# One token tile's attention input: transposes on the tensor engine replaced by transposing transfers, and the attention bias asked for behind them

## The chip, the cores and the metric

The kernel runs on one core of a Trainium2 chip. A core has five engines with an instruction stream each: TensorE (PE in the profile; PEld is its weight load), VectorE (DVE), ScalarE (ACT), GpSimd (POOL) and SyncE (SP), which issues most transfers. Each stream is worked off in order, and an instruction whose input is missing holds up all that stand behind it on its engine. Transfers run on 16 DMA engines. The metric is the device time of one launch in microseconds, as the median of several runs.

## What is computed

A trunk of two layers over 256 tokens of width 1024: each layer is a feed-forward part, a mixer and a second feed-forward part, each between two root-mean-square norms, on a residual stream h. The mixer of the first layer is a gated linear recurrence, that of the second an attention whose keys, values and forget-gate sums come from the stream after the first layer. Cut to the second layer:

```python
f = swiglu(rms_norm(h, ffn1_pre_g[1]), ffn1_w_gate[1], ffn1_w_up[1], ffn1_w_down[1])
h = h + 0.5 * rms_norm(f, ffn1_post_g[1])
hn = rms_norm(h, mix_pre_g[1])
m = forgetting_attention(hn, attn_w_q[0], attn_w_o[0], k, v, c)
h = h + rms_norm(m, mix_post_g[1])

def forgetting_attention(xq, w_q, w_o, k, v, c):
    q = (xq @ w_q).reshape(Bn, S, 16, 64).transpose(0, 2, 1, 3) * 64 ** -0.5
    ...
    logits = q_block @ k^T + c_query - c_key, masked to earlier tokens
    p = softmax(logits); o = p @ v
    return o.reshape(Bn, S, 1024) @ w_o
```

## The kernel before

**Tiles and operands.** The 256 tokens are two tiles t = 0 and 1 of 128, and h is kept as two tiles with tokens on the partitions. A product needs its input with features on the partitions: eight k tiles of 128 features each, for each token tile. float32 precision is reached by splitting every operand into a rounded high part and the remainder: a step of a product is three matmuls, high by high, high by low, low by high. The two parts of the current input are `xhi` and `xlo` (k tile, token), those of the weights `whi` and `wlo`. A weight is loaded into one of five `raw` buffers by SP (lines 161 and 164), rounded by ScalarE (line 173) and subtracted by VectorE (line 177); the subtraction frees the buffer.

**The order of work.** All weight pieces are a list of items. An item has a preparation (load and split) and its work for t = 0 and for t = 1, called halves. TensorE runs what is emitted in the order of emission. The other engines' streams are put together by a scheduler from readiness and priority (`tc.high_priority()` makes instructions urgent; inside one such region each engine keeps the order of emission), except that `tc.keep_in_program_order(x)` ties x behind the instruction that was emitted last before it on the same engine. After each half comes `tick()`: it counts down the list `pend`, where `defer(n, f)` puts f to be called at the (n + 1)th tick from there, and it prepares a further item.

**Into a stage.** `enter(t, ...)` stands at the end of a stage: it norms the product, adds it to h (line 311) and readies the next stage's input. For the stage looked at here, the attention's query product after the second layer's first feed-forward part, `inputs()` is deferred by `wait=3` and runs, for t = 1, after the third query half of t = 0. It transposes the eight 128 x 128 blocks of h on TensorE into two PSUM banks (`to_tp`, line 226), multiplies them by the gain (line 234), copies them to `xhi` (line 235) and subtracts for `xlo` (line 240), each in two pieces of four k tiles; `stat(t)` then forms the row norm (lines 205, 198, 200).

At other places in the kernel the second four k tiles take another way (`by_transfer`). `planes` (line 212, GpSimd) sorts the 32-bit words into two planes of 16-bit halves, `swap` (line 216) turns them with a transposing transfer on SP, in program order, and `join` (line 220, GpSimd) puts the halves together again. `turned_to_x` (lines 258, 259 and 240) makes the two operands, the multiplication and the high copy in program order.

**Attention.** Its order is written out by hand in `ATT_ORDER`:

```python
ATT_ORDER = ("0 0 0 0 0 0 0 l0 0 1 n0 l0 1 1 t0 n0 1 l0 v0 1 t0 n0 l0 1 v0 n0 1 t0 l1 1 ...
```

A digit is a half of t = 0 or t = 1; the first eight halves of each are the query product (items of two k tiles each, four items for the first eight heads, then four for the rest). `l0` are logits of tile 0: the step computes those of eight heads, adds the bias and takes the row maxima (VectorE, lines 1203 to 1208), and takes eight exponentials (ScalarE, line 1210); `n` norms them, `t` transposes them (line 1223) and `v` multiplies by the values (line 1237). After the fourth half the queries of the first heads are scaled (`heads_T`, line 1044, tile `htok`). For t = 0 they are turned on TensorE (line 1057, copied at line 1059), two ticks later; for t = 1 they are turned by planes, swap and join (lines 212, 216, 220), and the first `l1` needs them. Tile 1's bias `bias1`, 2 MB in SBUF, is read by `l1` only. It is loaded from DRAM by GpSimd's queue in `att_rows`, called just ahead of the first query half.

Of the kernel before, what the change touches and what calls it, by code (L numbers as in the profile page):

```python
# [9 lines left out]
F32 = mybir.dt.float32  # L10
F32R = mybir.dt.float32r
BF16 = mybir.dt.bfloat16
U16 = mybir.dt.uint16
AF = mybir.ActivationFunctionType
# [3 lines left out]
P = 128  # L18
# [25 lines left out]
def trunk_kernel(ctx: ExitStack, tc: tile.TileContext, A: dict, out: bass.AP):  # L44
    nc = tc.nc
# [5 lines left out]
    hpool = ctx.enter_context(tc.tile_pool(name="h", bufs=1))  # L51
# [6 lines left out]
    def nm(s):  # L58
        uid[0] += 1
        return f"{s}_{uid[0]}"  # L60
# [4 lines left out]
    def gtbank():  # L65
        return psum.tile([P, 512], F32, tag="gt", name=nm("gt"), bufs=2)
# [14 lines left out]
    def defer(n, fn):  # L81
        pend.append([n, fn])
# [23 lines left out]
    h = [hpool.tile([P, D], F32, tag=f"h{t}", name=f"h{t}") for t in range(2)]  # L106
# [23 lines left out]
    gT = cpool.tile([P, 56], F32, name="gT")  # L130
# [64 lines left out]
    def rstd_of(ss, n, f=1.0, add=nc.gpsimd):  # L195

        v = spool.tile([P, 1], F32, tag="nv", name=nm("nv"))
        add.tensor_scalar(v, ss[:, 0:1], ss[:, 1:2] if n == 2 else 0.0, D * EPS * f * f, ALU.add, ALU.add)  # L198
        r = spool.tile([P, 1], F32, tag="rstd", name=nm("rstd"), bufs=8)
        nc.gpsimd.tensor_tensor(r, v, mhalf, ALU.pow)  # L200
        return r

    def square_sum(src, acc, f=1.0):
        junk = spool.tile([P, D], BF16, tag="junk", name=nm("junk"), bufs=1)
        nc.scalar.activation(junk[:, :src.shape[1]], src, AF.Square, scale=f, accum_out=acc)  # L205

    def new_ss():
        return spool.tile([P, 2], F32, tag="ss", name=nm("ss"))

    def planes(dst, src):  # L210

        nc.gpsimd.tensor_copy(dst.rearrange("p (h f) -> p h f", h=2), src.bitcast(U16).rearrange("p (f h) -> p h f", h=2))

    def swap(turned, halves):

        tc.keep_in_program_order(nc.sync.dma_start(turned.rearrange("p (a b) -> p a b", b=P), halves, transpose=True))

    def join(dst, turned):

        nc.gpsimd.tensor_copy(dst, turned.rearrange("p (h f) -> p h f", h=2))  # L220

    def to_tp(src, n):

        tp = gtbank()
        for j in range(4):
            nc.tensor.transpose(tp[:, j * P:(j + 1) * P], src[:, n * 512 + j * P:n * 512 + (j + 1) * P], ident)  # L226
        return tp
# [10 lines left out]
    def x_lower(xg, dest, n):  # L238
        gi, xh, xl = dest
        nc.vector.tensor_tensor(xl[:, 4 * n:4 * n + 4, :], xg, xh[:, 4 * n:4 * n + 4, :].bitcast(F32), ALU.subtract)  # L240

    def to_x(tps, dest):

        with tc.high_priority():
            xg = [x_upper(tp, dest, n) for n, tp in enumerate(tps)]
            for n, v in enumerate(xg):
                x_lower(v, dest, n)

    def turned_to_x(v, dests, more):

        with tc.high_priority():
            xs = []
            for i, (gi, xh, xl) in enumerate(dests):
                xg = v if i == len(dests) - 1 else more()
                g = gT[:, gi + 4:gi + 8].unsqueeze(2).to_broadcast([P, 4, P])
                xs.append(xg.rearrange("p (a b) -> p a b", a=4))
                tc.keep_in_program_order(
                    nc.vector.tensor_tensor(xs[i], v.rearrange("p (a b) -> p a b", a=4), g, ALU.mult))
                tc.keep_in_program_order(nc.scalar.activation(xh[:, 4:, :], xs[i], AF.Copy))
            for xg, dest in zip(xs, dests):  # L260
                x_lower(xg, dest, 1)

    def to_x_tiles(tps, dest):

        gi, xh, xl = dest

        def operands(k):
            return tps[k // 4][:, k % 4 * P:(k % 4 + 1) * P], gT[:, gi + k:gi + k + 1]
        with tc.high_priority():
            for k in range(8):  # L270
                src, g = operands(k)
                nc.scalar.activation(xh[:, k, :], src, AF.Copy, scale=g)
            for k in range(8):
                src, g = operands(k)
                nc.vector.scalar_tensor_tensor(xl[:, k, :], src, g, xh[:, k, :].bitcast(F32), ALU.mult, ALU.subtract)
# [4 lines left out]
    def stat(t):  # L280
        ss = new_ss()
        square_sum(h[t], ss[:, 0:1])
        rs[t] = rstd_of(ss, 1)

    def enter(t, dests, pf, gb, half, last=False, normed=False, wait=3, spare=None):

        f = 1.0 / 16 if half else 1.0 / 32
        ss = new_ss()
        t1 = []
        urgent = tc.high_priority()  # L290
        urgent.__enter__()
        for n in range(2):
            square_sum(pf[n], ss[:, n:n + 1], f)
        for n in range(2):
            if n == 1 and last:
                r = rstd_of(ss, 2, f, nc.vector)
            t1.append(hpool.tile([P, 512], F32, tag="t1", name=nm("t1"), bufs=2))
            nc.vector.tensor_tensor(t1[n], pf[n], gb[:, n * 512:(n + 1) * 512], ALU.mult)
        if not last:
            r = rstd_of(ss, 2, f)  # L300

        sp, aq = nc.sync, nc.scalar
        pieces = [(n * 512, 512, None) for n in range(2)]
        if last:
            pieces = ([(0, 1024, sp)] if t == 0 else
                      [(0, 256, sp), (256, 256, aq), (512, 256, sp), (768, 256, aq)])
        for c, m, q in pieces:
            hn = h[t][:, c:c + m]
            for a in range(c, c + m, 512):
                n = min(m, 512)  # L310
                nc.vector.scalar_tensor_tensor(h[t][:, a:a + n], t1[a // 512][:, a % 512:a % 512 + n], r[:, 0:1],
                                               h[t][:, a:a + n], ALU.mult, ALU.add)
            if last:
                q.dma_start(out[0, t * P:(t + 1) * P, c:c + m], hn)
        urgent.__exit__(None, None, None)
        if last:
            return

        by_transfer = (spare or t == 1) and not (half and (len(dests) == 1 or t == 0)) and not normed
        if by_transfer:  # L320
            a = spare() if t == 0 else hpool.tile([P, 512], F32, tag="t1", name=nm("hp"), bufs=2)
            with tc.high_priority():
                planes(a.bitcast(U16), h[t][:, 512:])

        def inputs():
            tps = [to_tp(h[t], n) for n in range(1 if by_transfer else 2)]
            for dest in dests:
                to_x(tps, dest)
            stat(t)
            if by_transfer:  # L330
                b = spare() if t == 0 else spool.tile([P, 512], F32, tag="junk", name=nm("ht"), bufs=1)
                with tc.high_priority():
                    swap(b.bitcast(U16), a.bitcast(U16))
                defer(0, lambda: join(a.bitcast(U16).rearrange("p (f h) -> p h f", h=2), b.bitcast(U16)))
                defer(1 + 2 * t, lambda: turned_to_x(a, dests, spare))

        def norm():
            with tc.high_priority():
                normed_x()

        def normed_x():
            ss = new_ss()
            for n in range(2):
                square_sum(h[t][:, n * 512:(n + 1) * 512], ss[:, n:n + 1])
            rs[t] = rstd_of(ss, 2)
            hn = []
            for n in range(2):
                hn.append(hpool.tile([P, 512], F32, tag="t1", name=nm("hn"), bufs=2))
                nc.vector.tensor_scalar(hn[n], h[t][:, n * 512:(n + 1) * 512], rs[t][:, 0:1], None, ALU.mult)

            def go():
                tps = []
                for n in range(2):
                    tp = gtbank()
                    for j in range(4):
                        nc.tensor.transpose(tp[:, j * P:(j + 1) * P], hn[n][:, j * P:(j + 1) * P], ident)
                    tps.append(tp)
                to_x_tiles(tps, dests[0])
            defer(6, go)

        if normed:
            norm()
            settled[0] = True
        else:
            defer(wait, inputs)

    def gain_bcast(src):
        gb = hpool.tile([P, D], F32, tag="gb", name=nm("gb"), bufs=1)
# [239 lines left out]
    pools = {}  # L608
# [364 lines left out]
    kv = {}  # L973
# [61 lines left out]
    def att_rows():  # L1035

        tc.keep_in_program_order(nc.scalar.activation(warm, mhalf, AF.Exp))
        tc.keep_in_program_order(nc.gpsimd.dma_start(att["bias1"], kv["bias1"]))

    def heads_T(ps, t, n, scale, dst):  # L1040

# [121 lines left out]
    att = {}  # L1163
# [341 lines left out]
```

## Time and profile before

| | us |
|---|---|
| median of 3 runs (964.70 to 964.91) | 964.89 |
| profiled execution | 965.18 |
| its span, first to last instruction | 963.5 |
| TensorE busy | 954.8 |
| VectorE busy | 646.0 |
| ScalarE busy | 527.5 |
| GpSimd busy | 236.5 |

The granted TensorE clock was 0.999 of full speed. Times in rows are microseconds from the first instruction. A row of the timeline gives start, length, engine, line, instruction, output tile and input tiles, sizes, count, and in brackets how long the engine stood idle before and what ended that. The chain of waits is followed back from the last instruction: at each step to what released it. The query product of tile 0 begins at 709.3 us, that of tile 1 at 722.8.

### The profile page before, as it was taken

What the parts mean: (1) busy time and instruction counts of PE and PEld (TensorE: products, weight loads), DVE (VectorE), ACT (ScalarE), POOL (GpSimd) and SP (SyncE); (2) the same over time, 40 slices, a digit from 0 to 9 for tenths busy, and PEclk for the clock granted to TensorE, in tenths of its full rate; (3) what the DMA queues carried; (4) which work ended last, traced back from release to release, by engine and by line L of the source; (5) the groups of instructions that cost most, each with busy time, mean ns of one, the idle gap of its engine ahead of it and who ended that gap; (6) DMA issues with size and microseconds to landing.
All of it is one profiled execution on the core that took longest, in us unless ns stands there. A gap on an engine that the chain in (4) does not pass through costs nothing.

```text
span 963.5 us, 12847 instructions
## 1 busy us (share of the span) xinstructions
PE 954.8 (99%) x4559; PEld 789.6 (82%) x4559; DVE 646.0 (67%) x845; ACT 527.5 (55%) x750; POOL 236.5 (25%) x229
## 2 busy tenths in 40 slices
PE   9999999999999999999999999999999999999997
PEld 6888888898878888888898888888887788888885
DVE  6758774578997756664686566665488876666642
ACT  7446454568986555444565445444366865444431
POOL 2812230130003323230023623224022133232200
PEclk9999999999999999999999999999999999999999
DMA  8788996485338687676559979879763478777731
GB/s 283 227 229 252 250 291 196 143 222 166 128 110 244 203 238 215 201 245 193 138 158 313 249 223 262 223 190 289 227 255 102 121 210 260 208 225 234 217 110 44
DMA packets 153158, 199.84 MB, mean 207 GB/s; under 512 B 71390, under 2 KB 90182, under 8 KB 152966
## 3 DMA queue, kind: packets, MB, share of 16 engines
q1 hardware_dynamic: 150406, 192.11, 67.4%
q0 software_dynamic: 2080, 6.38, 2.3%
q8 instruction: 36, 0.59, 0.2%
q10 hardware_dynamic: 608, 0.53, 0.2%
q14 instruction: 28, 0.23, 0.1%
HBM read 182.19 MB, written 3.16 MB: 192 GB/s over the span
## 4 chain that ended last, share of the span: by engine, by line
PE 95%; DVE 2%; ACT 1%; issue 1%; POOL 0%; DMA 0%; POOLq 0%; DVEq 0%; ACTq 0%
PE mm L454 16%; PE mm L455 16%; PE mm L458 16%; PE mm L183 13%; PE mm L185 13%; PE mm L184 13%; PE gt L824 2%; PE mm L1340 1%; PE mm L190 1%; PE mm L191 1%; PE mm L192 1%; ACT pe L1210 1%; PE gt L226 1%; PE tr L127 0%; DVE wlo L177 0%
## 5 line engine op out<-in xcount | busy, mean ns | idle before, releaser
L177 DVE TENSOR_TENSOR wlo<-raw,whi 128x1024 fp32r<-128x1024 f32 (+5 forms) x329 | 423.0, 1293 | 213.9 <-ACT whi L173 212.4
L173 ACT ACTIVATE whi<-raw 128x1024 fp32r<-128x1024 f32 (+5 forms) x329 | 341.6, 1045 | 295.8 <-PE mm L458 107.2
L454 PE MATMUL mm<-whi,xhi 128*128 128x512 f32 x656 | 256.7, 391 | 0.0
L455 PE MATMUL mm<-wlo,xhi 128*128 128x512 f32 x656 | 255.5, 389 | 0.0
L458 PE MATMUL mm<-whi,xlo 128*128 128x512 f32 x656 | 202.2, 389 | 0.0
L454 PEld LDWEIGHTS mm<-whi,xhi 128*128 128x128 f32 x656 | 123.2, 188 | 25.9 <-issue 0.7
L458 PEld LDWEIGHTS mm<-whi,xlo 128*128 128x128 f32 x656 | 123.1, 188 | 26.0 <-DVE xlo L240 0.2
L455 PEld LDWEIGHTS mm<-wlo,xhi 128*128 128x128 f32 x656 | 123.2, 188 | 25.3 <-DVE wlo L177 0.3
L183 PE MATMUL mm<-whi,hhi 128*128 128x512 f32 x352 | 137.2, 390 | 0.0
L185 PE MATMUL mm<-whi,hlo 128*128 128x512 f32 x352 | 137.0, 389 | 0.0
L184 PE MATMUL mm<-wlo,hhi 128*128 128x512 f32 x352 | 137.0, 389 | 0.0
L569 POOL COPY pl<-prod 128x1024 uint16<-128x1024 uint16 (+1 forms) x48 | 67.7, 1410 | 168.9 <-DMA prod<-pl 168.9
L556 POOL COPY pl<-prod 128x1024 uint16<-128x1024 uint16 (+1 forms) x48 | 70.1, 1460 | 141.8 <-DVE prod L553 74.4
L185 PEld LDWEIGHTS mm<-whi,hlo 128*128 128x128 f32 x352 | 66.1, 188 | 13.7
L183 PEld LDWEIGHTS mm<-whi,hhi 128*128 128x128 f32 x352 | 66.1, 188 | 13.7
L184 PEld LDWEIGHTS mm<-wlo,hhi 128*128 128x128 f32 x352 | 66.1, 188 | 13.6
L198 POOL TENSOR_SCALAR nv<-ss 128x1 f32<-128x1 f32 x22 | 11.4, 517 | 252.8 <-ACT junk L205 252.8
L553 DVE SCALAR_TENSOR_TENSOR prod<-mm,rstd,sil 128x512 f32<-128x512 f32 (+1 forms) x48 | 33.7, 703 | 29.1 <-PE mm L458 24.8
L544 ACT ACTIVATE sil<-mm,rstd 128x512 f32<-128x512 f32 (+1 forms) x48 | 31.1, 650 | 32.4 <-PE mm L458 24.8
L575 DVE TENSOR_TENSOR hlo<-pl,hhi 128x512 fp32r<-128x512 f32 (+1 forms) x48 | 41.2, 858 | 3.6 <-ACT hhi L574 3.6
L183 PE MATMUL mm<-whi,xhi 128*128 128x512 f32 (+1 forms) x112 | 42.8, 382 | 0.0
L185 PE MATMUL mm<-whi,xlo 128*128 128x512 f32 (+1 forms) x112 | 42.5, 379 | 0.0
(235 smaller groups left out, 1067.8 us busy)
## 6 DMA issues: line engine op xcount, KB each, us to landing
raw<-in_ffn_w_down_dram SPq DMA_DIRECT2D x88, 512.0 KB
raw<-in_ffn_w_up_dram SPq DMA_DIRECT2D x80, 512.0 KB
raw<-in_ffn_w_gate_dram SPq DMA_DIRECT2D x78, 512.0 KB
raw<-in_rg_w_in_dram SPq DMA_DIRECT2D x10, 504.0 KB
raw<-in_rg_w_out_dram SPq DMA_DIRECT2D x10, 504.0 KB
raw<-in_ffn_w_gate_dram SPq DMA_DIRECT2D x19, 256.0 KB
raw<-in_ffn_w_up_dram SPq DMA_DIRECT2D x16, 256.0 KB
raw<-in_rg_w_in_dram SPq DMA_DIRECT2D x8, 512.0 KB
```

The costliest lines, as they stand in the source:

```text
L173: up = nc.scalar.activation(hi[:parts, c:c + m], rawv[:, c:c + m], AF.Copy)
L177: nc.vector.tensor_tensor(lo[:parts, c:c + m], rawv[:, c:c + m], hi[:parts, c:c + m].bitcast(F32), ALU.subtract)
L183: nc.tensor.matmul(ps, xh, wh, start=first, stop=False)
L184: nc.tensor.matmul(ps, xh, wl, start=False, stop=False)
L185: nc.tensor.matmul(ps, xl, wh, start=False, stop=last)
L454: nc.tensor.matmul(ps, get_x(t, k)[0], u.hi[:, c], start=k == 0, stop=False)
L455: nc.tensor.matmul(ps, get_x(t, k)[0], u.lo[:, c], start=False, stop=False)
L458: nc.tensor.matmul(ps, get_x(t, k)[1], u.hi[:, c], start=False, stop=k == nk - 1)
L553: nc.vector.scalar_tensor_tensor(pr[:, :nn], ps, rs[t][:, 0:1], s, ALU.mult, ALU.mult)
L556: nc.gpsimd.tensor_copy(halves.rearrange("p (h f) -> p h f", h=2), pr[:, :nn].bitcast(U16).rearrange("p (f h) -> p h f", h=2))
L569: nc.gpsimd.tensor_copy(halves.rearrange("p (f h) -> p h f", h=2), turned.rearrange("p (h a) b -> p h (a b)", h=2))
L575: keep(nc.vector.tensor_tensor(lv, x, hv.bitcast(F32), ALU.subtract))
```

## The change

For this one stage and for t = 1 (`whole`: after a feed-forward part, one destination, not the first stage), all eight k tiles go by planes, swap and join, and `turned_to_x` is called once for k tiles 0 to 3 and once for 4 to 7, with a new argument n. The planes are emitted in `enter`; the rest in `whole_inputs`, at the tick at which `inputs` ran. The turned halves use two of the four buffers of `pT`, which hold queries and turned probabilities in attention. The two calls of `turned_to_x` are due four and five ticks later, after the seventh and the eighth half of t = 0. The load of `bias1` is deferred to the eighth tick after `att_rows`, also after the eighth half.

```diff
-    def turned_to_x(v, dests, more):
+    def turned_to_x(v, dests, more, n=1):
...
-                g = gT[:, gi + 4:gi + 8].unsqueeze(2).to_broadcast([P, 4, P])
+                g = gT[:, gi + 4 * n:gi + 4 * n + 4].unsqueeze(2).to_broadcast([P, 4, P])
...
-                tc.keep_in_program_order(nc.scalar.activation(xh[:, 4:, :], xs[i], AF.Copy))
+                tc.keep_in_program_order(nc.scalar.activation(xh[:, 4 * n:4 * n + 4, :], xs[i], AF.Copy))
             for xg, dest in zip(xs, dests):
-                x_lower(xg, dest, 1)
+                x_lower(xg, dest, n)
...
+        whole = half and len(dests) == 1 and t == 1 and not normed
+        if whole:
+            with tc.high_priority():
+                hp = [hpool.tile([P, 512], F32, tag="t1", name=nm("hp"), bufs=2) for _ in range(2)]
+                for n in range(2):
+                    planes(hp[n].bitcast(U16), h[t][:, n * 512:(n + 1) * 512])
...
+        def whole_inputs():
+            ht = [pools["a"].tile([P, 512], F32, tag="pT", name=nm("ht"), bufs=4).bitcast(U16) for _ in range(2)]
+            with tc.high_priority():
+                for n in range(2):
+                    swap(ht[n], hp[n].bitcast(U16))
+            stat(t)
+            with tc.high_priority():
+                for n in range(2):
+                    join(hp[n].bitcast(U16).rearrange("p (f h) -> p h f", h=2), ht[n])
+            for n in range(2):
+                defer(3 + n, lambda n=n: turned_to_x(hp[n], dests, None, n))
...
-            defer(wait, inputs)
+            defer(wait, whole_inputs if whole else inputs)
...
-        tc.keep_in_program_order(nc.gpsimd.dma_start(att["bias1"], kv["bias1"]))
+        defer(7, lambda: tc.keep_in_program_order(nc.gpsimd.dma_start(att["bias1"], kv["bias1"])))
```

## The prediction

> **What bounds the kernel now.** I read the page first, then the chain of waits around the change, then the engines one by one in that stretch.
>
> ```profile
> span 963.5 us, 12847 instructions
> PE 954.8 (99%) x4559; PEld 789.6 (82%) x4559; DVE 646.0 (67%) x845; ACT 527.5 (55%) x750; POOL 236.5 (25%) x229
> PE 95%; DVE 2%; ACT 1%; issue 1%; POOL 0%; DMA 0%; POOLq 0%; DVEq 0%; ACTq 0%
> ```
>
> TensorE is the bound: 99% busy and 95% of the chain. An instruction taken off it is worth its full time, and nothing else is worth anything unless TensorE comes to wait for it. The chain of waits from the third query half of token tile 0 to the logits of token tile 1 (start, length, what):
>
> ```profile
> 713.05 0.46 PE mm L458 x2
> 713.51 0.87 PE gt L226 x8
> 714.38 0.23 PE mm L454
> ...
> 722.54 0.47 PE mm L458 x2
> 723.03 0.75 DVE htok L1044
> 723.78 0.08 DVE mx L1208
> 723.93 0.27 issue
> 724.19 2.12 ACT pe L1210 x11
> 726.31 0.50 ACT qT L1059
> 726.81 0.76 ACT pe L1210 x4
> 727.57 0.96 ACT whi L173
> 728.55 0.91 DVE wlo L177
> ...
> 729.70 0.76 DVE htok L1044
> ...
> 730.57 1.91 POOL pl L212
> 732.50 3.07 DMA htok<-pl
> 735.62 1.69 POOL qT L220
> 737.35 1.14 PE gt L1194 x8
> ```
>
> Two things are to be seen. The eight transposes of token tile 1 take 0.87 us of TensorE's chain. And from 723 to 737 us the chain is not TensorE's at all: it runs over ScalarE's eight exponentials (723.9 to 727.6), the query tile (htok), its transposing transfer and the copy after it. TensorE just reaches the logits of tile 1 as that chain ends. So this stretch has no slack to take in a late input.
>
> **The change, part by part.** *Removed from TensorE*: the eight transposes, 0.87 us, all of it on the chain. With them goes the reading of their PSUM banks; the multiplications by the gain, the copies to the high part and the subtractions remain, two of each, moved later:
>
> ```profile
> 711.51 1.41 DVE L311 SCALAR_TENSOR_TENSOR h<-t,rstd,h 128x512 f32<-128x512 f32 x2
> 715.11 1.28 DVE L234 TENSOR_TENSOR xg<-gt,gT 128x512 f32<-128x512 f32 x2
> 715.83 1.23 ACT L235 ACTIVATE xhi<-xg 128x512 fp32r<-128x512 f32 x2 [1.66 <-DVE xg L234]
> 716.97 1.28 DVE L240 TENSOR_TENSOR xlo<-xg,xhi 128x512 fp32r<-128x512 f32 x2
> 722.83 0.40 PE L454 MATMUL mm<-whi,xhi 128*128 128x512 f32 x1
> 725.93 0.48 PE L454 MATMUL mm<-whi,xhi 128*128 128x512 f32 x1
> 728.77 0.62 PE L458 MATMUL mm<-whi,xlo 128*128 128x512 f32 x2
> ```
>
> Before, the operands were complete at 718.3 and first used at 722.83, the first query half of tile 1 (it reads k tiles 0 and 1): 4.6 us of slack. Its third half, from 725.93, is the first to read k tiles 4 to 7; its fourth ends at 729.39. Less 0.87, the first two dates become 721.96 and 725.06.
>
> *Added: two plane copies and two joins on GpSimd, two transposing transfers on SP.* The same chain exists for half a tile in another stage; on GpSimd:
>
> ```profile
> 305.12 1.97 POOL L212 COPY hp<-h 128x1024 uint16<-128x1024 uint16 x1 [1.51 <-DVE h L311]
> 312.03 1.34 POOL L220 COPY hp<-ht 128x1024 uint16<-128x1024 uint16 x1 [2.84 <-DMA ht<-hp]
> ...
> 714.26 1.01 POOL L198 TENSOR_SCALAR nv<-ss 128x1 f32<-128x1 f32 x1 [2.15 <-ACT junk L205]
> 715.37 0.56 POOL L200 TENSOR_TENSOR rstd<-nv,mhalf 128x1 f32<-128x1 f32 x1
> ```
>
> From the end of the plane copy to the start of the join: 312.03 - 307.09 = 4.94 us. In the chain above the same transfer took 3.07 us. I keep both. Here the first half of the residual row is written at 712.2. Plane copies 712.3 to 714.2 and 714.2 to 716.2; transfers from 714.2 and 716.2; first landing 717.3 to 719.2, the second 2 us later; first join to 718.7 at best (the norm's sum and root, 1.6 us in the last two rows, may come between) or 720.5, second join by 720.7 to 722.6. Gain multiplication 0.64, high copy 0.63: k tiles 0 to 3 are there between 720.0 and 721.8, against 721.96. **The first half is just in time**, so its transfer costs nothing by itself.
>
> *Moved behind: the second half's input.* This is the step that I expect to fail. The gain multiplication and the high copy are both kept in program order, which ties each behind the instruction last emitted before it on its engine. For k tiles 0 to 3 that is the copy of tile 0's turned queries, long done. But the call for k tiles 4 to 7 is due one half later, after the eighth half of tile 0, and between the two stands the first logit step. Its last ScalarE instruction is the eighth exponential. So the high copy of k tiles 4 to 7 stands **behind all eight exponentials**, and its multiplication behind tile 0's second htok.
>
> ```profile
> 721.44 0.29 DVE L1203 CUSTOM_DVE_ANT_0 pe<-gt,bias 128x128 f32<-128x128 f32 x1 [3.19 <-PE gt L1194]
> 723.88 0.41 ACT L1210 ACTIVATE pe<-pe,mx 128x128 f32<-128x128 f32 x1 [4.28 <-DVE mx L1208]
> 727.09 0.39 ACT L1210 ACTIVATE pe<-pe,mx 128x128 f32<-128x128 f32 x1
> ```
>
> The exponentials start once VectorE has the row maxima, behind htok, which waits for the eighth half. Less 0.87 they start at 723.01. VectorE's 3.2 us gap ahead of the first logit pass (first row) now closes: the first multiplication and subtraction, 0.64 us each, fall between 719 and 722.7, at or in the logit passes (from 720.6), and delay the maxima by 0 to 1.3 us; I take 0.75, since the multiplication mostly precedes them and the subtraction does not. The eight exponentials take 3.69 us with the query copy of 0.5 us among them as now, 3.2 without; I take 3.45. Then the high copy, 0.63.
>
> - Middle: 723.01 + 0.75 + 3.45 + 0.63 = 727.84, against the third half's start of 725.93 before: **+1.9 us**.
> - Low: 723.01 + 3.2 + 0.63 = 726.84: +0.9 us.
> - High: 723.01 + 1.28 + 3.69 + 0.63 = 728.61: +2.7 us.
>
> These shifts contain the 0.87 us gained. Behind the waiting third half stand on TensorE the transposes of the first probabilities, the fourth half, and through it tile 1's first htok. That htok began at 729.70, 0.3 us after its last matmul (729.39), since VectorE was in a weight subtraction; started at once it gives 0.3 us back. The chain htok, planes, transfer, join, logits then carries the rest into TensorE: **+1.6 us**, from +0.6 to +2.4.
>
> VectorE and GpSimd also slow each other, which can raise this end:
>
> ```profile
> L177 DVE TENSOR_TENSOR wlo<-raw,whi x329: 817/1225/2324, 17.7 to 937.9; 128x1024 fp32r<-128x1024 f32 x146, 128x1008 fp32r<-128x1008 f32 x5, 126x1024 fp32r<-126x1024 f32 x5, 128x680 fp32r<-128x680 f32 x4
> ```
>
> The same subtraction takes 1.23 us in the median and 2.32 at most, 1.1 us more. I leave that to the range's upper end, as most of them show nothing of it.
>
> The Trainium skill, "SBUF — State Buffer", section "SBUF: two separate sides", says that a VectorE operation with two SBUF inputs and a GpSimd operation that reads SBUF exclude each other for a whole instruction. By that rule the first subtraction, in the time of the second join, waits up to a join's length; with the 1.1 us above the sum would be +2.7, or 967.6. Row and rule do not contradict each other, but the median row says that meeting is the exception.
>
> *Moved: the bias tile's transfer*, 2 MB, from the head of this stretch to behind the second join on GpSimd.
>
> ```profile
> 711.49 0.63 POOL L1038 DMA_DIRECT2D bias<-bias1d  x1
> DMA to landing us min/median/max: 11.8/11.8/11.8
> 711.00:723.30 12.30, 12.30 (x73) 10.05 (x72) 8.95 (x24) 4.84 (x8) 2.68 (x4) 1.00 0.92 370
> 723.30:729.80 6.50, 6.50 (x39) 5.20 (x39) 4.28 (x14) 5.92 (x20) 0.00 (x0) 1.00 0.04 18
> ```
>
> (The last two: stretch, length, busy time of PE, PEld, DVE, ACT, POOL, clock, DMA share, GB/s.) It ran while the DMA engines were 92% busy, and left them idle from 723 to 730. Asked for at 721 to 722.6, it fits that hole: 2.1 MB at 370 GB/s is 5.7 us, so it is there by 728.5, and by 734.4 even at the old 11.8 us. Its reader is the logit pass after 737.35. Cost nothing; its cover is 3 us at worst.
>
> *SP.* Its issues in this stretch:
>
> ```profile
> 714.13 16.01 SPq L164 DMA_DIRECT2D raw<-in_attn_w_o_dram  x3
> SPq L164 <- DVE wlo L177: 22.3, 7, 14.2
> ```
>
> Three weight loads, the last of which blocks SP for 14.2 us until a raw buffer is freed at 729.8. The two transfers have to be ahead of it. They are tied only behind loads emitted earlier (this load is emitted long after), are urgent, and are ready at 714 and 716: I count them ahead, at no cost; a load moved behind them is not needed before 727.
>
> **Sum.** The profiled execution has 965.18 us for a span of 963.5, and the median of the runs is 964.89, 0.3 lower. 965.18 + 1.6 = 966.8 in a profile, and **966.5** by the median.
>
> **Rivals.**
> *Full gain.* If the high copy is early after all (the order among ScalarE's instructions turns out looser than I read it, or the exponentials start earlier), nothing waits: 964.89 - 0.87 = 964.0; with up to 0.3 us from htok, 963.7. For it: the input is multiplied by 723. Against it: the tie behind the exponentials.
> *Bias collision (slower).* The bias transfer, begun at 722, is still running when tile 1's queries are turned at about 734, and that transfer takes 4.94 instead of 3.07 us, straight in the chain: 966.5 + 1.9 = 968.4. It decides if the bias takes longer than its old 11.8 us. Against it: the idle hole; for it: the weight loads at 730 to 734.
> *SP blocked (slower).* The transfers stand behind the blocked weight load: issue at 730.1, landing 733.2, join 734.6, multiplication and copy 735.9, against 722.83: +13 us, 978. Decided by the order on SP alone; the ties speak against it.
>
> **How the numbers follow.** Forecast 0.5, full gain 0.2, collision (or VectorE and GpSimd in each other's way to the same size) 0.19, SP 0.06, and 0.05 for a gain elsewhere by a shifted order. The range 963.7 to 968.8 holds the first three; the forecast's own is 965.5 to 967.3. By 0.2%, 1.93 us, about what this measurement tells from no change, the bounds are 962.96 and 966.82. The forecast lies over the upper one in somewhat under half of its cases: slower 0.22 + 0.25 = 0.47, faster 0.05, the same 0.48.
>
> **What would show it.** Right: no transposes at the former 713.5, two transposing transfers near 714 and 716, the high copy of k tiles 4 to 7 after the last exponential near 727.2, and TensorE waiting 2 to 3 us ahead of tile 1's third query half for that copy. Wrong: that copy among or before the exponentials; a wait at the first query half for the first input (the transfers or joins late); a bias transfer that lands after 735; or tile 1's logits starting earlier than 737.

## The result, and the profile after

| | before | changed kernel |
|---|---|---|
| median of 6 runs each, us | 964.87 (964.32 to 964.91) | 969.87 (969.08 to 971.04) |
| ratio, 95% interval | 1 | 1.0054 (1.0044 to 1.0064) |
| profiled execution, us | 965.18 | 969.08 |
| its span, us | 963.5 | 967.4 |
| mean granted TensorE clock | 0.999 | 0.997 |

The change costs 5.0 us; 1.6 were forecast, with 968.8 as the upper end of the range. Single runs of the kernel before lie some 1.9 us above the rest now and then (4 of the 32 in the second series of experiments, at an unchanged clock), so medians are compared. The page of the changed kernel still shows TensorE 99% busy, with its busy time hardly changed:

```profile
span 967.4 us, 12835 instructions
PE 955.2 (99%) x4551; PEld 789.6 (82%) x4551; DVE 648.7 (67%) x845; ACT 527.6 (55%) x750; POOL 241.7 (25%) x233
PE 93%; DVE 2%; ACT 2%; issue 1%; POOL 1%; POOLq 0%; DVEq 0%; ACTq 0%
```

Busy time rose by 0.4 us although eight transposes are gone, and the chain's share on TensorE fell from 95% to 93%. So TensorE waits somewhere, and some of its work takes longer. When two profiles are laid side by side, their origins have to be compared first: here the addition to h starts at 710.72 in place of 711.51. These 0.79 us lie ahead of the change and are noise of the start (in the traces of the experiments this date lies between 710.66 and 711.43); they have to be added to every date of the changed kernel.

TensorE's timeline of the changed kernel at tile 1's query halves (first half, end of the second, third):

```profile
721.37 0.39 PE L472 MATMUL mm<-whi,xhi 128*128 128x512 f32 x1
...
723.63 0.62 PE L476 MATMUL mm<-whi,xlo 128*128 128x512 f32 x2
724.09 0.60 PE L1075 MATMUL tr<-ident,htok 128*128 128x128 f32 x4
728.30 0.50 PE L472 MATMUL mm<-whi,xhi 128*128 128x512 f32 x1 [3.61 <-ACT xhi L259]
```

The first and second half wait for nothing. The third stands still for 3.61 us, for the high copy of k tiles 4 to 7. The chain of waits shows why that copy is late:

```profile
716.81 1.31 POOL hp L220
718.13 0.03 issue
718.15 1.82 DVE hp L258
719.98 0.02 issue
720.00 0.64 ACT xhi L259
...
722.70 0.66 DVE htok L1062
723.36 0.60 DVE hp L258
723.96 0.09 DVE mx L1226
724.04 0.02 issue
724.07 1.26 ACT pe L1228 x6
...
726.00 1.73 ACT pe L1228 x9
727.73 0.53 ACT xhi L259
```

Its multiplication (DVE hp at 723.36) is done at 723.96, and 0.6 us more would do. But the copy stands behind the eight exponentials and is worked off at 727.7. Ahead of that, the first multiplication took 1.82 us: GpSimd's second join ran from 718.1. The exponentials start at 724.07, as the last row maxima (mx) are ready. ScalarE was free hardly earlier, since it rounded a weight until 723.99, which the kernel before does after the exponentials:

```profile
722.93 1.06 ACT L173 ACTIVATE whi<-raw 128x1024 fp32r<-128x1024 f32 x1 [2.29 <-PE mm L476]
```

What TensorE does after its wait is seen in the windows (stretch, length, busy time of TensorE, granted clock, DMA share, GB/s):

```profile
716.00:724.00 8.00, 7.99 (x48) 1.00 0.98 301
724.00:728.30 4.30, 0.70 (x6) 1.00 0.83 318
728.30:730.00 1.70, 1.70 (x6) 0.71 0.26 106
730.00:732.00 2.00, 2.00 (x8) 0.50 0.32 49
732.00:734.00 2.00, 2.00 (x17) 0.89 0.56 213
734.00:740.00 6.00, 6.00 (x45) 1.00 0.55 131
```

For some four microseconds behind the wait the clock is at 0.71, 0.50 and 0.89. Work lost: 1.70 x 0.29 + 2.00 x 0.50 + 2.00 x 0.11 = 1.7 us. In the kernel before it was 1.00 throughout this stretch. Together: -0.87 + 3.61 + 1.71 = +4.45 us. By the dates, tile 1's first logits moved from 737.35 to 741.02 + 0.79 = 741.81, by 4.46 us. So close a match is in part luck, since 0.24 us for which TensorE waited here before, for tile 1's queries, are gone: in the changed kernel these are ready at 739.82, 1.2 us ahead of the logits. In the two profiles the whole kernel grew by 3.9 + 0.79 = 4.7 us. The profile is that of the fastest of the six runs; the other five have a mean clock of 0.995 or 0.996 in place of 0.997, so the clock may have cost more in them, which no trace shows.

The transfers, on SP and by the list of issues:

```profile
713.06 3.21 SPq L216 DMA_TRANSPOSE ht<-hp  x2
716.37 14.44 SPq L164 DMA_DIRECT2D raw<-in_attn_w_o_dram  x4
```

```profile
bias<-bias1d POOLq DMA_DIRECT2D x1, 2048.0 KB, 8.7
```

Both transposing transfers are issued ahead of the blocked weight load. The bias tile, asked for at 719.4, lands 8.7 us later, long ahead of its reader.

### The profile page after: what moved, and what is told of

Read it like the earlier page. It is cut to its first block, busy times and chain, and to the rows that moved or that the text cites. A ratio compares the mean times of both kernels' runs of the same rounds, so it can differ in the third digit from the quotient of the medians.

```text
span 967.4 us, 12835 instructions
## 1 busy us (share of the span) xinstructions
PE 955.2 (99%) x4551; PEld 789.6 (82%) x4551; DVE 648.7 (67%) x845; ACT 527.6 (55%) x750; POOL 241.7 (25%) x233
## 3 DMA queue, kind: packets, MB, share of 16 engines
HBM read 182.19 MB, written 3.16 MB: 192 GB/s over the span
## 4 chain that ended last, share of the span: by engine, by line
PE 93%; DVE 2%; ACT 2%; issue 1%; POOL 1%; POOLq 0%; DVEq 0%; ACTq 0%
PE mm L472 16%; PE mm L473 16%; PE mm L476 16%; PE mm L183 13%; PE mm L185 12%; PE mm L184 12%; PE gt L842 2%; PE mm L1358 1%; PE mm L190 1%; PE mm L191 1%; PE mm L192 1%; ACT pe L1228 1%; DVE pe L1221 1%; DVE wlo L177 0%; PE tr L127 0%
```

## The experiments

Each was timed against the kernel before, on the same chip. The differences below are to that kernel's median in the same runs (964.57 for the first four, 964.56 for the second four, 964.78 for the last three); the changed kernel's is +5.00. The theories: A, the tie of the high copy behind the exponentials stops TensorE, and the stop costs clock too; B, the bias tile's later transfer; C, GpSimd's copies and VectorE's operations in each other's way; D, which came up after the first four, is told below.

**e1_no_tie.** The tie taken from the one copy; the planner then puts it ahead of the exponentials.

```diff
...
-                tc.keep_in_program_order(nc.scalar.activation(xh[:, 4 * n:4 * n + 4, :], xs[i], AF.Copy))
+                up = nc.scalar.activation(xh[:, 4 * n:4 * n + 4, :], xs[i], AF.Copy)
+                if tie:
+                    tc.keep_in_program_order(up)
...
```

(`tie` is false for k tiles 4 to 7 at this place alone.)

> The changed kernel without one tie: the high copy of k tiles 4 to 7 is no longer kept behind the instruction emitted before it on ScalarE, and stands ahead of the eight exponentials in ScalarE's stream. Theory A (that copy behind the exponentials stops TensorE for 3.6 us, and the stop costs 1.7 us more in granted clock): TensorE's wait ahead of tile 1's third query half falls from 3.6 to under 0.5 us, the clock stays at 1.00, and the time is 964.0 to 964.8 us. Theory B (the bias tile's later transfer is what costs): 969 to 970. Theory C (the added plane copies and joins on GpSimd and VectorE's operations block each other): 968 to 970, since all of them are still there.

Measured: 966.45, +1.88 us (ratio 1.002, 1.0011 to 1.0029). The greater part of the loss, 3.1 of 5.0 us, is gone with this one edit, so A is right about most of it; B and C alone are out. But A foretold a gain, and 1.9 us of loss are left. On TensorE:

```profile
725.77 0.50 PE L474 MATMUL mm<-whi,xhi 128*128 128x512 f32 x1 [0.39 <-ACT xhi L259]
...
727.74 0.73 PE L478 MATMUL mm<-whi,xlo 128*128 128x512 f32 x2 [0.77 <-DVE xlo L240]
728.82 0.63 PE L1243 MATMUL tr<-ident,pe 128*128 128x128 f32 x4 [0.35 <-DVE pe L1237]
```

Three short waits instead of a long one, all for ScalarE's and VectorE's work of these microseconds: high copy, low part, tile 0's probabilities.

**e2_earlier_call.** `defer(3 + n, ...)` becomes `defer(2 + n, ...)`, ties kept.

> Both calls of turned_to_x one tick earlier (after the sixth and the seventh half of tile 0), all ties kept; the second then is emitted ahead of the first logit step. Theory A: no wait of TensorE ahead of tile 1's query halves over 0.3 us, 963.9 to 964.5 us, the 0.87 us of the transposes gained. Theory B: 969 to 970. Theory C: 968 to 970.

Measured: 967.95, +3.38 us (1.0026 to 1.0051). No theory had this. The wait has moved to another place. TensorE, then the chain:

```profile
722.44 1.26 PE L1212 MATMUL gt<-kT,qT 64*128 64x128 f32 x16 [2.89 <-ACT qT L1077]
```

```profile
721.18 0.04 ACT xhi L259
...
721.71 0.59 ACT qT L1077
722.30 0.14 issue
722.44 1.26 PE gt L1212 x16
```

One tick earlier, the first high copy comes ahead of the copy of tile 0's queries, whose transposes had ended at 718.2: ScalarE stands before its input, the logits stand behind the queries, and TensorE waits 2.89 us. It is the same fault with the parts exchanged. My edit did not test A alone, as I had meant it to.

**e3_filled_wait.** Matmuls without use laid into the wait of the changed kernel: a step `b` behind tile 1's second query half.

```diff
+        if c == "b":
+            keep_busy(16)
```

> The changed kernel with 16 matmuls of constants (bfloat16, 128x512, results unused) between tile 1's second and third query half, about 3.4 us of TensorE work laid into its wait. If the low clock (0.71, 0.50 and 0.89 after the wait) comes from TensorE standing still: the third half starts no later than before, the clock stays at 1.00 behind it, and the time falls by 1.7 us or more, to 966.5 to 968.2, with a spread under 0.7 us in place of 2. If the low clock has another cause: 969.9 as before, or more.

Measured: 968.11, +3.54 us (1.0028 to 1.0053), 1.5 less than the changed kernel; 1.7 or more was foretold. Timeline and windows (all engines' busy times, then clock, DMA share, GB/s):

```profile
724.83 3.66 PE L127 MATMUL tr<-const-bfloat16-1.0 128*128 128x512 bf16 x16
728.76 0.50 PE L472 MATMUL mm<-whi,xhi 128*128 128x512 f32 x1 [0.26 <-ACT xhi L259]
```

```profile
728.80:732.00 3.20, 3.20 (x16) 2.44 (x16) 2.47 (x4) 2.31 (x3) 0.00 (x0) 1.00 0.23 81
732.00:736.00 4.00, 4.00 (x37) 3.13 (x36) 3.75 (x22) 0.98 (x5) 1.04 (x1) 1.00 0.82 232
```

The third half starts no sooner, yet the clock stays at 1.00 and the median is lower. The low clock is the price of standing still. The intervals of this ratio and of the changed kernel's overlap, so the trace carries this more than the times. Four of the five runs lie within 0.71 us; one, 970.51, does not.

**e4_bias_alone.** The last hunk of the change on the kernel before.

> The kernel before, with the bias tile's transfer alone moved behind the eighth half of tile 0. Theory A: no change, 964.6 to 965.2 us. Theory B: 969 to 970. Theory C: no change.

Measured: 964.58, +0.01 us (0.9990 to 1.0008). B is out.

What is left of 1.9 us in the first experiment led to **theory D**: in the kernel before, the gain multiplications and subtractions lay in a gap of VectorE (715 to 718, idle from there to 721.4); by transfer those of the first half come 4 us later and those of the second 8 or more, into the time in which VectorE works off tile 0's logits, and that chain, exponentials, probabilities, tile 1's queries, has no slack.

**e5_same_tick.** Both calls at the eighth tick (`defer(3, ...)`): behind the query copy, ahead of the exponentials.

> The changed kernel with both calls of turned_to_x at the eighth tick, after the seventh half of tile 0: behind tile 0's first query copy on ScalarE (which the second experiment had put behind the first high copy) and ahead of the eight exponentials. Theory A (nothing but an in-order tie stops TensorE): no wait over 0.5 us at tile 1's query halves nor ahead of the first logits, 963.9 to 964.6 us. Theory D (A, and besides the four operand instructions of VectorE now fall into the time in which tile 0's logits are worked off, so that chain, and tile 1's queries behind it, come 1.5 to 2 us later whatever the ties): 965.8 to 967.0, as in the first experiment.

Measured: 966.31, +1.75 us (1.0010 to 1.0028), as by D. The trace is that of the fastest of its eleven runs, 965.26. No query half waits in it; TensorE waits for tile 0's probabilities, and the exponentials begin at 724.17 with the addition to h at 710.68, 1.1 us later than before on the same axis. They follow the last row maxima at once.

```profile
PE tr L1241 <- DVE pe L1235: 0.9, 1, 0.9
PE gt L1212 <- POOL qT L220: 0.6, 1, 0.6
```

**e6_logits_later.** The first logit step one place later.

```diff
-    ATT_ORDER = ("0 0 0 0 0 0 0 l0 0 1 n0 l0 1 1 t0 ...
+    ATT_ORDER = ("0 0 0 0 0 0 0 0 l0 1 n0 l0 1 1 t0 ...
```

> The changed kernel with the first logit step one place later in the written order, behind the eighth half of tile 0 in place of the seventh; all ties and ticks as in the changed kernel. The call for k tiles 4 to 7 is then emitted ahead of the exponentials. Theories A and D: TensorE's wait of 3.6 us ahead of tile 1's third query half is gone and the clock stays at 1.00; by A 964 to 965 us, by D 966 to 967.5, since the logits of tile 0 begin a half (1.36 us) later still. If the tie is not what stops TensorE: 969 to 970.5.

Measured: 967.32, +2.76 us (1.0021 to 1.0040). The high copy comes ahead of the exponentials, and the wait at the third half is gone, as by A and D. The logits, a half later, now let TensorE wait for their probabilities:

```profile
PE tr L1241 <- DVE pe L1235: 2.7, 1, 2.7
```

**e7_join_on_act.** The first experiment with the second join on ScalarE, so that no GpSimd copy runs beside the first multiplication.

```diff
...
+                    tc.keep_in_program_order(nc.scalar.activation(
+                        hp[1].bitcast(U16).rearrange("p (f h) -> p h f", h=2),
+                        ht[1].rearrange("p (h f) -> p h f", h=2), AF.Copy))
...
```

> The first experiment with one more edit: the second join is made by ScalarE, which stands idle there, in place of GpSimd, so that no GpSimd copy runs beside the first gain multiplication (1.7 us in place of 0.69 in the first experiment). If that meeting is on the path (part of D): the multiplication takes 0.7 us, the first logit pass starts 1 us earlier, and the time falls by 0.6 to 1.0 us, to 965.4 to 965.9. If not: 966.2 to 966.7.

Measured: 965.88, +1.32 us (1.0008 to 1.0026), 0.56 less than the first experiment and just inside what was foretold. The multiplication, by VectorE's timeline in the first experiment and here:

```profile
719.37 1.70 DVE L258 TENSOR_TENSOR hp<-hp,gT 128x512 f32<-128x512 f32 x1 [1.92 <-POOL hp L220]
```

```profile
718.42 0.69 DVE L258 TENSOR_TENSOR hp<-hp,gT 128x512 f32<-128x512 f32 x1 [1.66 <-POOL hp L220]
```

The intervals of the two ratios overlap, so the traces rather than the times carry this: the same multiplication takes 1.01 us less when no join runs beside it. The exponentials gain only half of that, beginning 13.68 us after the addition to h in place of 14.19, about the 0.56 us of the times. C is a part of the loss.

**e8_half_only.** Only k tiles 4 to 7 by transfer, k tiles 0 to 3 as before, with the bias tile moved.

> Only k tiles 4 to 7 go by transfer at this place, k tiles 0 to 3 stay with TensorE (four transposes less); one plane copy, one transfer, one join, the call at the eighth tick, the bias tile behind the eighth half. Theory A: 964.57 - 0.44 = 964.1 us. Theory D: half of the operand work stays in VectorE's gap ahead of the logits and there is no second join to meet, so the loss is under 0.5 us: 964.0 to 964.7. Either way not above 965.

Measured: 965.06, +0.50 us (0.9994 to 1.0011): no difference that can be told, and no gain either. It is the best of the versions with a transfer at this place.

**e9_two_more_ops** and **e10_four_more_ops.** The kernel before, with VectorE work without use among tile 0's first logit passes; no other edit.

```diff
+                if t == 0 and g == 0:
+                    scr = hpool.tile([P, 512], F32, tag="t1", name=nm("scr"), bufs=2)
+                    for _ in range(2):
+                        nc.vector.tensor_tensor(scr, pe.rearrange("p a b -> p (a b)"), h[1][:, :512], ALU.mult)
```

(4 in place of 2 in the second.)

> The kernel before, transposes on TensorE and all, with two more VectorE multiplications of 128x512 (0.69 us each, result unused, reading the first logits) laid among tile 0's first logit passes, ahead of the row maxima. No transfer, no GpSimd work, no bias move. Theory D (VectorE's work in that time is on the path): the exponentials start 1.2 to 1.4 us later and the time grows by 0.8 to 1.4 us, to 965.4 to 966.0. If that chain has slack: 964.4 to 964.8.

> The same with four multiplications, 2.76 us. Theory D: the growth doubles, 966.6 to 967.4. With slack: under 965.

Measured: 965.91, +1.13 us (1.0007 to 1.0025), and 968.12, +3.34 us (1.0016 to 1.0038). Without any transfer, two operations of 0.69 us at this place cost 1.1 us, and TensorE waits for the same thing as in e5:

```profile
PE tr L1227 <- DVE pe L1221: 1.0, 1, 1.0
PE gt L1194 <- POOL qT L220: 0.3, 1, 0.3
```

So there is no slack here, as D says. But the edit did more than D says: it also changed the order on ScalarE. The planner put a weight rounding ahead of the exponentials, as in the changed kernel:

```profile
723.92 1.06 ACT L173 ACTIVATE whi<-raw 128x1024 fp32r<-128x1024 f32 x1 [4.80 <-PE mm L458]
724.89 0.38 ACT L1214 ACTIVATE pe<-pe,mx 128x128 f32<-128x128 f32 x1
```

The traces together, as delays against the kernel before, all counted from the addition to h, in us:

| | row maxima that the first exponential needs | first exponential | end of the kernel |
|---|---|---|---|
| e5 | 1.12 | 1.12 | 0.9 |
| e6 | 2.45 | 2.45 | 2.5 |
| e1 | 1.35 | 1.82 | 1.8 |
| e9 | 0.95 | 1.49 | 1.2 |
| e7 | 0.09 | 1.31 | 1.3 |

The end moves about as far as the first exponential. In e5 and e6 VectorE's maxima make the whole delay, as D has it. In the others a part is ScalarE's own: the untied high copy in e1, the rounding in e9, and in e7, where the maxima are hardly late, both. No run takes the rounding out alone, so its price is read from the traces and not tested.

In e10 four operations cost more than double, which was not foretold. In its trace the exponentials begin 3.3 us later, only 1.55 us of it by the maxima; two weight roundings stand ahead of them, and TensorE's longest wait is 2.4 us, at an undiminished clock. Three of the seven runs, that of the trace among them, are at 966.6 to 966.9, as foretold, the others at 968.1 to 968.8, mostly at a lower mean clock (0.997 against 0.998 to 0.999). In those a wait may have cost clock too, or they may be the scatter that the kernel before has as well; no trace of one of them shows which.

**e11_bias_in_front.** The changed kernel with the bias tile's transfer where it was.

> The changed kernel with the bias tile's transfer back at the head of the stage, where it was. If the bias's later transfer costs anything (theory B) this is faster than 969.9. By A and D it is not: the two transposing transfers then run beside 2 MB of bias, land up to 2 us later and the operands with them, so 969.5 to 972.

Measured: 973.53, +8.75 us (1.0071 to 1.0099), more than foretold. GpSimd's second join and TensorE's wait:

```profile
725.41 1.32 POOL L220 COPY hp<-ht 128x1024 uint16<-128x1024 uint16 x1 [6.99 <-DMA ht<-hp]
```

```profile
PE mm L472 <- ACT xhi L259: 7.5, 1, 7.5
```

Beside 2 MB of bias the second transposing transfer keeps GpSimd waiting for 6.99 us, and the second join starts 14.4 us after the addition to h in place of 7.4. Moving the bias tile costs nothing and saves the change 3.7 us: that half of the change does what it is for.

## Why the prediction was wrong

The forecast was a loss of 1.6 us; it was 5.0. The wait that was forecast came, and the sign was right; the size was wrong by two terms, of 1.1 and 1.7 us. With the 1.6 they make 4.4 of the 4.7 us of the profiles.

- *The transposes, -0.87 us.* Right: tile 0's fourth half follows the third at once.
- *The first half just in time.* Right, with little to spare: its high copy was ready at 720.63, used at 721.37.
- *The high copy behind all eight exponentials.* Right. It ran directly after the last one, TensorE waited for it and nothing else, and e1 shows that this tie alone makes 3.1 of the 5.0 us. The forecast had a wait of 1.9 + 0.87 = 2.8 us here; it was 3.6.
- *The start of the exponentials: 723.01 + 0.75.* **The first failed term.** They started at 724.07 + 0.79 = 724.86, 1.1 us later than my 723.76. Two things that the sum had at nothing delayed them, and ended within 0.05 us of each other. On VectorE I had let the multiplication "mostly precede" the logit passes at 0.64 us; it took 1.81, because it met the second join on GpSimd. In e7, without that meeting, the row maxima are ready 12.43 us after the addition to h in place of 13.32. I had quoted the row that gives this price (2.32 against 1.23 us for a subtraction) and left it to the range's upper end "as most of them show nothing of it". That was the wrong reading of a median: GpSimd is busy for 25% of the span, so most of those subtractions met nothing, whereas this multiplication waits for the first join, and the second follows that join at once, so here the meeting was built in. On ScalarE I had kept the order of the kernel before; in the changed one a weight rounding stands ahead of the exponentials until 723.99, so that without the meeting alone they would have started at most 0.08 us earlier. My 0.75 us for VectorE was near by luck: without the meeting the maxima come 0.96 us late (e7), but the second multiplication, 0.60 us of the chain between htok and the last maxima, had no term in it. The Trainium skill's rule that I weighed ("SBUF — State Buffer", "SBUF: two separate sides") was right in kind and about right in size, though it struck the first multiplication in place of the subtraction: 1.1 us more beside a join of 1.35 us. With it the sum was 967.6, still 2.3 us short.
- *The exponentials, 3.45 us.* 3.56, right.
- *TensorE at full clock after its wait.* **The second failed term, and the one that was missing altogether.** I charged a wait at its length and had no term for the clock. It cost 1.7 us more by the granted clock, and e3, which fills the wait and does not shorten it, gets 1.5 us back. The Trainium skill has this too ("TensorE: Matmul & The Clock Gate", section "Why this matters for your kernels"): no idle gaps over about 3 us, or the clock falls to half. The trace agrees: 0.50 for two microseconds after 3.61 us. With a forecast wait of 2.8 us I stood at its edge and should have priced it: in e2's trace 2.89 us were enough, in e6's 2.66 us were not.
- *SP ahead of the blocked load; the bias tile at no cost.* Right (713.06 and the list of issues; e4). The two rivals that hung on these are out. The collision of the bias with tile 1's queries did not come: their transfer took 3.16 us.
- *0.3 us given back by tile 1's htok, whose chain carries the rest into TensorE.* The first is right: htok began 0.04 us after its last matmul (733.39 after 733.35). The second is not: tile 1's queries were ready 1.2 us ahead of their logits, which came late by TensorE's own wait and clock.

What I had not seen is theory D: even untied, the change loses. I counted VectorE's four operations only as a delay of the exponentials in the tied case, and let the "full gain" rival have 964.0 once the copy was early. e1, e5 and e7 are that rival, and they lose 1.3 to 1.9 us: the late operand work meets the one chain that has no slack, as the prediction itself had read off the chain of waits, and the new order on ScalarE adds to it. A chance of 0.2 for a full gain contradicted my own first reading.

## What to carry to other kernels

Moving work off the bound engine pays only if what it fed still arrives in a gap: ask for each instruction of the new path not just whether it is in time for its reader, but whose turn it takes on the in-order engines. A tie in program order is a wait: name what stands ahead of it on its engine, at the moment at which it is emitted. Read the streams of the other engines anew as well: here the planner moved a weight rounding that no edit names. And price a wait of the tensor engine with its clock: in the traces here waits of 2.9 and 3.6 us cost about half as much again.

## What the runs showed of the hardware that was not expected

- **The clock after a wait.** 3.61 us of waiting: 0.71, 0.50, 0.89 over the following 6 us, 1.7 us of work lost. 7.5 us of waiting (e11): 0.55, 0.50 and 0.67 over the three stretches of 4 us from 728, the wait's end included. Waits between 2.4 and 2.9 us do not always cost it: in e2's profile, after 2.89 us, the clock was 0.84, 0.50 and 0.81 over three stretches of 2 us from 722 (again 1.7 us of work lost), in e6's, after 2.66 us, it stayed at 1.00. With the clock the time varied: e6's runs at a mean clock of 0.999 took 966.6 to 967.4 us, those at 0.997 took 968.4 to 969.7.
- **GpSimd and VectorE.** A GpSimd copy beside a multiplication with two inputs in SBUF stops the one or the other, and which one is not settled in these kernels, where the two start within a few hundredths of a microsecond. In the changed kernel and the first experiment the multiplication took longer (1.81 and 1.70 us in place of 0.69); in e5 the joins did, in VectorE's timeline and GpSimd's:

```profile
718.12 0.69 DVE L258 TENSOR_TENSOR hp<-hp,gT 128x512 f32<-128x512 f32 x1 [1.41 <-POOL hp L220]
```

```profile
716.73 3.28 POOL L220 COPY hp<-ht 128x1024 uint16<-128x1024 uint16 x2
```

In the changed kernel the two joins took 2.71 us. That profile of e5 is the fastest of its eleven runs (965.26 to 968.67); whether this race makes their spread was not tried.
